# Three tiny tiles padded so that every large on-chip tile starts at a multiple of 64 bytes

## The chip, the cores and the metric

The kernel runs on one core of a Trainium2 chip. The metric is the device time of one execution in microseconds, a median over runs. One further execution was taken with the hardware profiler; all rows below are from it. The engines are PE (TensorE: matrix products), DVE (VectorE), ACT (ScalarE), POOL (GpSimd) and SP (SyncE, which here only issues transfers).

## The reference

A trunk of two decoder layers on a sequence of 512 tokens with model width 1024, all in float32. Layer 0 mixes tokens by stick-breaking attention (16 heads of width 64), layer 1 by retention (4 heads); each is followed by a squared-ReLU MLP with hidden width 4096, and there is an RMS norm before every sub-layer and at the end.

```python
def stick_breaking_attention(h, w_in, w_out):
    q, k, v = jnp.split(h @ w_in, 3, axis=-1)
    ...
    z = jnp.einsum('bhqd,bhkd->bhqk', qb, kp) * scale
    log_keep = jnp.where(mask, jax.nn.log_sigmoid(-z), 0.0)
    later = lax.cumsum(log_keep, axis=3, reverse=True) - log_keep
    a = jnp.where(mask, jnp.exp(jax.nn.log_sigmoid(z) + later), 0.0)
    outs.append(jnp.einsum('bhqk,bhkd->bhqd', a, vp))
    ...
    return o @ w_out

def reference(x, ...):
    h = x
    for layer in range(DEPTH):
        hn = rms_norm(h, g_mix[layer])
        h = h + (stick_breaking_attention if layer % 2 == 0 else retention)(hn, ...)
        h = h + squared_relu_mlp(rms_norm(h, g_mlp[layer]), ...)
    return rms_norm(h, g_final)
```

## The kernel before

Every float32 operand of a product is split into a rounded part (`hi`) and the rest (`lo`), and each product is made of three: hi by hi, hi by lo, lo by hi (`mm3_steps`, issued at line 79). The activations lie transposed (features on the 128 partitions, 512 tokens along the row), so nearly all products move 512 columns past a stationary block of 128 by 128. In the rows a product is written `out<-moving,stationary`: `so<-o,whi_so` moves the attention's output `o` past the output projection's weights, `up<-xhi,whi_up` moves the normed activations `x` past the MLP's first weights.

All products are tied into one hand-written order on PE. Layer 0 runs so: `v` (values for all heads), then `q` and `k` chains of 24 products, with the heads' work laid between pieces of them. Each head has its scores `z` (11 products: three add a mask, four move `k`, four move the split key tile `khi`, in widths 128 to 512; `weights_of`), two sigmoids on ACT, a running product and a multiplication on DVE, ten transposes `t` (line 82; the stationary operand is the weights tile `sg`) and eight products `av` that move the transposed weights `ahi` and `alo` (`turned`, `mixed`). From the 14th head on, the output projection `so` takes the place of the chains: a group of 96 products over four PSUM banks and four chains of 24, 192 in all, which move nothing but `o`. Then follow the MLP, retention (scores `rs`, its products `ro`, its output projection `rout`) and the second MLP.

On-chip memory is handed out by pools that are opened and closed like a stack. The pools `const`, `hp` (`h` and `x`), `wp` (weights: `raw`, `whi`, `wlo`) and `small` stay open to the end. On top of them lies in turn the attention's pool `sb`, the MLP's `mlp0`, retention's `ret` and `mlp1`. A tile takes its size rounded up to 32 bytes per partition, and the next one starts right behind it. In `small` lies `ssq`, of 32 bytes, and what comes behind it starts 32 bytes past a multiple of 64: the small scalars, and then every tile of the attention's pool (`q`, `k`, `hi`, `lo`, `keep`, `sg`, `ahi`, `alo`, the `vo` ring with `v` and `o`). In the MLP's pool this holds for `hT` alone, as `r2`, again 32 bytes, stands right behind it; in retention's for `cs` alone, as `minus` stands right behind it. The tiles of `const`, `hp` and `wp`, and all other large tiles, start at multiples of 64.

Of the kernel before, what the change touches and what calls it, by code (L numbers as in the profile page):

```python
# [7 lines left out]
F32 = mybir.dt.float32  # L8
# [4 lines left out]
P = 128  # L13
D = 1024
S = 512
KT = D // P
NB = S // P
# [7 lines left out]
def trunk_kernel(  # L25
# [28 lines left out]
    small = ctx.enter_context(tc.tile_pool(name="small", bufs=2))  # L54
# [484 lines left out]
    def mlp_s(layer, norm, early=None, first_up=None):  # L539
# [15 lines left out]
        with ExitStack() as st:  # L555
            mp = st.enter_context(tc.tile_pool(name=f"mlp{layer}", bufs=2, reuse_waits="tile"))
            hT = mp.tile([P, NB, D], F32, name="hT", bufs=1)
            finish = early is not None
            r2 = mp.tile([P, 2, NB], F32, name="r2", bufs=1)
            us = {}  # L560
            left, right = slice(0, 512), slice(512, D)
            low, high = slice(0, S // 2), slice(S // 2, S)
# [241 lines left out]
                    nxt.add(d)  # L804


            ssq = small.tile([P, NB, 2], F32, tag="ssq", name=f"ssq{layer}", bufs=1)
            scales = {}

            def squares(b, j):  # L810
# [71 lines left out]
    def ret_layer(norm0, norm1, early):  # L882
        w = w_ret_in
        with ExitStack() as st:
            rp = st.enter_context(tc.tile_pool(name="ret", bufs=2, reuse_waits="tile"))
            cs = rp.tile([P, 2, S], F32, name="cs", bufs=1)
            nc.scalar.dma_start(cs, rot)
            minus = rp.tile([P, KT], F32, name="minus", bufs=1)
            nc.vector.tensor_scalar(minus, gain[:, 2, :], -1.0, None, op0=ALU.mult)

            def ring(name, dtype=F32):
# [341 lines left out]
    norm, nxt = nxt, Norm("n2")  # L1233
    early = Steps(side_by_side())
    mlp_s(0, norm, early, first_up)
    norm, nxt = nxt, Norm("n3")
    ret_layer(norm, nxt, early)
    norm = nxt
    mlp_s(1, norm)


# [52 lines left out]
```

## Time and profile before

| | |
|---|---|
| median of 3 runs | 1334.22 us (1331.64 to 1334.32) |
| the profiled execution's own time | 1334.43 us |
| its span, first to last instruction | 1332.6 us |
| PE busy | 1301.3 us, 98% of the span |
| DVE, ACT, POOL busy | 71%, 49%, 11% |
| granted PE clock, mean over the span | 0.992 |

The span is what the trace shows; the 1.8 us between it and the execution's time lie before the first and after the last instruction. PE's products overlap each other by some 160 ns (a product's record lasts 389 ns, and the next one starts 227 ns after it), so the pace of PE is read from starts, not from durations.

### The profile page before, as it was taken

Reading aid. Unit: us, or ns where it says so; the run is one execution under the profiler, and the core shown is the slowest. Engines: PE = TensorE matmul, PEld = TensorE weight load, DVE = VectorE, ACT = ScalarE, POOL = GpSimd, SP = SyncE. Lnnn points to the kernel's source line nnn. Section 1 sums busy time; section 2 is a strip of 40 time slices with the busy share of each in tenths; the row PEclk is TensorE's granted clock in tenths of the full one; section 3 lists DMA queues with packets and bytes.
Section 4 is the critical chain, followed back from the end, with each engine's and each line's share of the span. In section 5 each row is a group of like instructions: output and inputs, shape, how many; then the busy total and the mean of one; then the engine's idle time right before and its main releaser. Section 6 shows DMA issues by size and latency. Waiting matters only on the chain.

```text
span 1332.6 us, 15884 instructions
## 1 busy us (share of the span) xinstructions
PE 1301.3 (98%) x5982; PEld 1076.4 (81%) x5982; DVE 939.7 (71%) x1206; ACT 652.1 (49%) x958; POOL 142.4 (11%) x162
## 2 busy tenths in 40 slices
PE   9999999999999999997999999999999999999996
PEld 7888878788888888776878788788788888888884
DVE  5778886735576575899787767677773657657588
ACT  6466664535555534554635235235254444553355
POOL 1000000110111111101011000000100011111113
PEclk9999999999999999998999999999999999999998
DMA  6455451554445354433536335334434344435324
GB/s 208 120 142 137 108 137 55 168 132 104 148 111 140 114 126 143 111 77 89 149 88 144 123 78 138 115 75 124 172 100 112 94 158 111 130 123 127 111 64 111
DMA packets 103437, 160.51 MB, mean 120 GB/s; under 512 B 6208, under 2 KB 43200, under 8 KB 103360
## 3 DMA queue, kind: packets, MB, share of 16 engines
q1 hardware_dynamic: 79648, 98.12, 23.8%
q0 software_dynamic: 22272, 58.73, 19.6%
q10 hardware_dynamic: 1440, 2.64, 0.5%
q8 instruction: 47, 0.77, 0.2%
q14 instruction: 30, 0.25, 0.1%
HBM read 146.88 MB, written 2.10 MB: 112 GB/s over the span
## 4 chain that ended last, share of the span: by engine, by line
PE 90%; DVE 7%; issue 1%; ACT 1%; DMA 1%; POOL 0%; POOLq 0%; DVEq 0%; ACTq 0%
PE up L79 26%; PE X L79 17%; PE Z L79 9%; PE k L79 7%; PE rout L79 6%; PE q L79 6%; PE Y L79 4%; PE so L79 3%; PE v L79 3%; PE z L79 2%; PE av L79 2%; PE ro L79 2%; PE t L82 1%; DVE hT L734 1%; PE rs L79 1%
## 5 line engine op out<-in xcount | busy, mean ns | idle before, releaser
L79 PE MATMUL up<-xhi,whi_up 128*128 128x512 f32 x512 | 200.1, 391 | 0.0
L79 PE MATMUL up<-xhi,wlo_up 128*128 128x512 f32 x512 | 199.4, 389 | 0.0
L79 PE MATMUL up<-xlo,whi_up 128*128 128x512 f32 x512 | 199.3, 389 | 0.0
L606 POOL DMA_DIRECT2D B<-in_w_mlp_down x92 | 82.7, 901 | 608.4 <-DVE b_1lo L110 274.1
L120 DVE TENSOR_TENSOR wlo_up<-raw_up,whi_up 128x1024 fp32r<-128x1024 f32 x64 | 78.1, 1220 | 78.1 <-ACT whi_up L119 78.0
L119 ACT CAST whi_up<-raw_up 128x1024 fp32r<-128x1024 f32 x64 | 67.4, 1052 | 95.5 <-PE up L79 82.0
L79 PEld LDWEIGHTS up<-xhi,wlo_up 128*128 128x128 f32 x512 | 96.1, 188 | 20.2
L79 PEld LDWEIGHTS up<-xhi,whi_up 128*128 128x128 f32 x512 | 96.1, 188 | 19.7
L79 PEld LDWEIGHTS up<-xlo,whi_up 128*128 128x128 f32 x512 | 96.1, 188 | 19.5
L110 DVE TENSOR_TENSOR b_1lo<-B,b_1hi 128x1024 fp32r<-128x1024 f32 x56 | 68.3, 1220 | 3.6 <-ACT b_1hi L109 3.3
L110 DVE TENSOR_TENSOR b_0lo<-B,b_0hi 128x1024 fp32r<-128x1024 f32 x56 | 68.4, 1221 | 2.3 <-ACT b_0hi L109 1.1
L109 ACT CAST b_0hi<-B 128x1024 fp32r<-128x1024 f32 x56 | 58.7, 1048 | 6.8 <-DVE B L646 2.6
L109 ACT CAST b_1hi<-B 128x1024 fp32r<-128x1024 f32 x56 | 58.8, 1050 | 6.6 <-DVE B L650 3.5
L591 ACT ACTIVATE U<-up 128x512 f32<-128x512 f32 x64 | 36.5, 592 | 37.6 <-PE up L79 37.6
L79 PE MATMUL q<-xlo,whi_q 128*128 128x512 f32 x128 | 51.5, 403 | 1.5 <-DVE xlo L264 1.5
L79 PE MATMUL k<-xhi,wlo_k 128*128 128x512 f32 x128 | 51.2, 400 | 0.0
L79 PE MATMUL q<-xhi,whi_q 128*128 128x512 f32 x128 | 50.8, 397 | 0.2 <-ACT xhi L263 0.2
L79 PE MATMUL k<-xlo,whi_k 128*128 128x512 f32 x128 | 50.8, 397 | 0.0
L79 PE MATMUL k<-xhi,whi_k 128*128 128x512 f32 x128 | 50.5, 395 | 0.0
L110 DVE TENSOR_TENSOR a_1lo<-S,a_1hi 128x512 fp32r<-128x512 f32 x24 | 16.5, 688 | 48.1 <-ACT a_1hi L109 48.1
L79 PE MATMUL q<-xhi,wlo_q 128*128 128x512 f32 x128 | 50.3, 393 | 0.0
L79 PE MATMUL rout<-yhi,whi_rout 128*128 128x512 f32 x128 | 50.1, 392 | 0.0
(389 smaller groups left out, 3349.3 us busy)
## 6 DMA issues: line engine op xcount, KB each, us to landing
B<-in_w_mlp_down POOLq DMA_DIRECT2D x96, 512.0 KB, 5.1
raw_up<-in_w_mlp_up SPq DMA_DIRECT2D x64, 512.0 KB, 3.9
B<-in_w_ret_in SPq DMA_DIRECT2D x24, 512.0 KB, 3.9
raw_rout<-in_w_ret_out SPq DMA_DIRECT2D x16, 512.0 KB, 3.6
raw_q<-in_w_sb_in SPq DMA_DIRECT2D x8, 512.0 KB, 4.4
raw_k<-in_w_sb_in SPq DMA_DIRECT2D x8, 512.0 KB, 4.3
q<-hi SPq DMA_DIRECT2D x32, 128.0 KB, 3.4
raw_so<-in_w_sb_out SPq DMA_DIRECT2D x8, 512.0 KB, 3.9
```

Source lines behind the costliest of these rows:

```text
L79: pe(nc.tensor.matmul(o, a, b, start=start, stop=stop, **kw))
L82: pe(nc.tensor.transpose(o, a, ident))
L109: nc.scalar.copy(hi, src_ap)
L110: (eng or nc.vector).tensor_tensor(lo, src_ap, hi.bitcast(F32), op=ALU.subtract)
L119: nc.scalar.copy(hi, raw)
L120: (sub or nc.vector).tensor_tensor(lo, raw, hi.bitcast(F32), op=ALU.subtract)
L591: nc.scalar.activation(U[:, m, :], banks[m], AF.Relu)
L606: nc.gpsimd.dma_start(t[:, ks, :], src[:, ks, :], **kw)
L734: nc.vector.scalar_tensor_tensor(at, acc[b], by, at, op0=ALU.mult, op1=ALU.add)
```

## The change

Three tiles get twice the bytes that they use, and their first half is used as before: `ssq` and `minus` take 64 bytes in place of 32, and `r2` takes 64 in place of 32.

```diff
@@ -556,7 +556,7 @@
             hT = mp.tile([P, NB, D], F32, name="hT", bufs=1)
             finish = early is not None
-            r2 = mp.tile([P, 2, NB], F32, name="r2", bufs=1)
+            r2 = mp.tile([P, 2, 2 * NB], F32, name="r2", bufs=1)[:, :, 0:NB]
@@ -804,7 +804,8 @@
-            ssq = small.tile([P, NB, 2], F32, tag="ssq", name=f"ssq{layer}", bufs=1)
+
+            ssq = small.tile([P, NB, 4], F32, tag="ssq", name=f"ssq{layer}", bufs=1)[:, :, 0:2]
@@ -885,7 +886,7 @@
-            minus = rp.tile([P, KT], F32, name="minus", bufs=1)
+            minus = rp.tile([P, 2 * KT], F32, name="minus", bufs=1)[:, 0:KT]
```

No instruction is added, removed or moved on any engine, and no shape changes. What changes is where tiles lie. Start bytes in the built programs, and what is left of them after division by 64:

| tile | before | after |
|---|---|---|
| `xhi0` (pool `hp`) | 34112, 0 | 34112, 0 |
| `whi` (pool `wp`), first buffer | 79168, 0 | 79168, 0 |
| `o0` (attention) | 147744, 32 | 147776, 0 |
| `q0_0` (attention) | 188704, 32 | 188736, 0 |
| `ahi_0_0` (attention) | 211232, 32 | 211264, 0 |
| `hT` (MLP) | 114464, 32 | 114496, 0 |
| `U0_0` (MLP) | 130880, 0 | 130944, 0 |
| `cs` (retention) | 114464, 32 | 114496, 0 |
| `dec0` (retention) | 118592, 0 | 118656, 0 |

## Rows read from the trace of the kernel before

**Rows 1.** The page: the span, the busy time of three engines with their share and number of instructions, and the shares of the chain of work that ended last, by engine.

```profile
span 1332.6 us, 15884 instructions
PE 1301.3 (98%) x5982; PEld 1076.4 (81%) x5982; DVE 939.7 (71%) x1206; ACT 652.1 (49%) x958; POOL 142.4 (11%) x162
...
PE 90%; DVE 7%; issue 1%; ACT 1%; DMA 1%; POOL 0%; POOLq 0%; DVEq 0%; ACTq 0%
```

**Rows 2.** PE's waits over the whole span: the waiting product, what released it, then us in total, times, longest.

```profile
PE rbps_n L79 <- DVE diag_n L252: 6.6, 1, 6.6
...
PE t L82 <- ACT sg L415: 2.1, 1, 2.1
...
PE z L79 <- DMA k<-lo: 1.2, 1, 1.2
```

**Rows 3.** PE's timeline inside the output projection: start in us, length in us, the products merged where neighbours are alike. In this stretch rows come in turn with one and with two products, so a row with two comes every three products.

```profile
231.97 0.63 PE L79 MATMUL so<-o,whi_so 128*128 128x512 f32 x2
...
234.77 0.63 PE L79 MATMUL so<-o,whi_so 128*128 128x512 f32 x2
```

**Rows 4.** The same timeline in the first MLP, one product in each row; between the two rows lie 25 more.

```profile
257.79 0.39 PE L79 MATMUL up<-xhi,whi_up 128*128 128x512 f32 x1
...
263.68 0.39 PE L79 MATMUL up<-xhi,wlo_up 128*128 128x512 f32 x1
```

**Rows 5.** Pieces of the chain that ended last, in order of time: start in us, us, what, number of products.

```profile
231.20 10.05 PE so L79 x43
...
627.16 5.44 PE X L79 x24
```

**Rows 6.** Groups of products that move 512 columns, over the whole span: number, busy us, mean ns of one, idle time before.

```profile
L79 PE MATMUL up<-xlo,whi_up 128*128 128x512 f32 x512 | 199.3, 389 | 0.0
...
L79 PE MATMUL so<-o,whi_so 128*128 128x512 f32 x128 | 42.2, 409 | 0.2 <-ACT whi_so L119 0.2
```

**Rows 7.** The output projection's tile `so`: shortest, median and longest duration in ns.

```profile
L79 PE MATMUL so<-o,whi_so x128: 388/396/632, 197.8 to 255.9; 128*128 128x512 f32 x128
...
L79 PE MATMUL so<-o,wlo_so x64: 392/395/632, 198.4 to 256.2; 128*128 128x512 f32 x64
```

**Rows 8.** The heads' products from 66 to 242 us, shapes kept apart: number, busy us, mean ns of one.

```profile
L79 PE MATMUL z<-hi,qlo 128*128 128x512 f32 x16 | 6.3, 395 | 0.0
L79 PE MATMUL av<-ahi,v 128*128 128x512 f32 x16 | 6.3, 395 | 0.0
L79 PE MATMUL av<-alo,v 128*128 128x512 f32 x16 | 6.3, 395 | 0.0
L79 PE MATMUL av<-alo,v 128*128 128x384 f32 x16 | 5.4, 340 | 0.0
L79 PE MATMUL z<-k,q 128*128 128x384 f32 x16 | 5.4, 337 | 0.0
...
L79 PE MATMUL av<-alo,v 128*128 128x256 f32 x16 | 4.5, 279 | 0.0
L79 PE MATMUL av<-alo,v 128*128 128x128 f32 x16 | 4.4, 274 | 0.0
```

**Rows 9.** Retention's scores from 640 to 650 us, whose tiles start at multiples of 64, in the same columns.

```profile
L79 PE MATMUL rs<-q0lo,k0hi 128*128 128x384 f32 x2 | 0.7, 338 | 0.0
...
L79 PE MATMUL rs<-q0lo,k0hi 128*128 128x256 f32 x2 | 0.6, 280 | 0.0
...
L79 PE MATMUL rs<-q0hi,k0lo 128*128 128x128 f32 x2 | 0.5, 274 | 0.0
```

**Rows 10.** PE's timeline behind transposes, in the second MLP (all tiles at multiples of 64); between the two rows lie four products.

```profile
1015.17 0.39 PE L79 MATMUL up<-xlo,whi_up 128*128 128x512 f32 x1
...
1016.33 0.39 PE L79 MATMUL up<-xhi,whi_up 128*128 128x512 f32 x1
```

**Rows 11.** The same behind a head's transposes in the attention, where the chain's own operands start at multiples of 64; between the two rows lie nine products.

```profile
101.94 0.40 PE L79 MATMUL q<-xhi,wlo_q 128*128 128x512 f32 x1
...
104.25 0.39 PE L79 MATMUL q<-xhi,whi_q 128*128 128x512 f32 x1
```

**Rows 12.** Stretches around the two places at which the granted clock is low: from and to in us, length, then busy us and instructions of PE, weight loads, DVE, ACT and POOL, granted clock (1.00 is 2.4 GHz), DMA share, GB/s.

```profile
195.20:197.10 1.90, 0.00 (x0) 0.00 (x0) 1.80 (x2) 1.90 (x6) 1.53 (x1) 1.00 0.97 280
...
198.50:202.00 3.50, 3.50 (x10) 2.72 (x9) 3.41 (x5) 0.29 (x2) 0.00 (x0) 0.51 0.49 112
...
611.10:617.70 6.60, 0.04 (x1) 0.03 (x1) 6.53 (x16) 1.55 (x2) 1.19 (x1) 0.53 0.00 0
617.70:621.80 4.10, 4.10 (x8) 2.60 (x9) 4.10 (x5) 1.86 (x3) 0.22 (x1) 0.50 0.00 0
```

**Rows 13.** PE's timeline in the first of these places; from the first row's start to the last row's lie six products.

```profile
198.61 1.06 PE L79 MATMUL so<-o,whi_so 128*128 128x512 f32 x2
...
201.17 0.99 PE L79 MATMUL so<-o,whi_so 128*128 128x512 f32 x2
```

**Rows 14.** Other engines, over the whole span: DVE's subtraction into a tile of the attention (`alo`) and into one of retention (`ylo`), and weight loads of transposes whose stationary tile is the attention's `sg` or retention's `y`.

```profile
L110 DVE TENSOR_TENSOR alo<-t,ahi 128x512 fp32r<-128x512 f32 x32 | 21.0, 681 | 3.4 <-ACT ahi L109 3.3
...
L82 PEld LDWEIGHTS t<-ident,sg 128*128 128x128 f32 x160 | 18.3, 140 | 4.5 <-ACT sg L415 2.3 <-DVE oF L465 0.2
...
L110 DVE TENSOR_TENSOR ylo<-yt,yhi 128x512 fp32r<-128x512 f32 x16 | 11.0, 688 | 10.6 <-ACT yhi L109 10.6
...
L82 PEld LDWEIGHTS yt<-ident,y 128*128 128x128 f32 x64 | 8.0, 140 | 2.1
```

## The prediction, made before the changed kernel ran

> **What bounds the kernel.** I read the page first: PE is busy for 98% of the span and holds 90% of the chain that ended last; no other engine is above 71% [rows 1]. PE's waits over the whole span are few: 6.6 us at one norm, 2.1 us for one head's transposes, 1.2 us for one transfer [rows 2]. So time that a product gives up on PE before one of these waits is time that the kernel gives up, as long as what ends the wait moves with PE. It does: the longest ones in the attention end with ACT work on PSUM banks that PE has just filled, and the norm's wait starts from PE's own last sums. A busy PE can still be a slow PE, so I next read its pace from starts in the timeline, in the stretches where like products follow each other.
>
> There the two kinds of tiles part. In the output projection, 12 products lie between the starts 231.97 and 234.77 [rows 3]: 2.80 us / 12 = 233.3 ns each. In the first MLP, 26 steps lie between 257.79 and 263.68 [rows 4]: 5.89 / 26 = 226.5 ns. The chain's pieces say the same over longer stretches: 43 products of `so` in 10.05 us are 233.7 ns, 24 of retention's `X` in 5.44 us are 226.7 ns [rows 5]. All move 512 columns past 128 by 128, all take weights from the same `whi` and `wlo` buffers or like ones, and PE waits for nothing in these stretches. The durations agree: medians of 396 and 395 ns in `so` [rows 7], against a mean of 389 in `up`. (The mean of 409 in `so` holds the products at the low clock [rows 6].) What `so` has apart from the others is that its moving tile `o` starts 32 bytes past a multiple of 64. The step is 233.3 - 226.7 = 6.7 ns, and at 2.4 GHz that is 16 cycles, the time of 16 columns, which are 64 bytes. I read this as one more piece of 64 bytes that a moving row touches when it starts in the middle of one: 33 pieces in place of 32.
>
> [...]
>
> **The change part by part.** No instruction comes or goes, so the sum is over products whose moving tile moves to a multiple of 64.
>
> *The output projection.* 128 + 64 = 192 products [rows 7]. Eight ran at the low clock, where six take 2.56 us, 427 ns each [rows 13], which is 512 columns at 1.2 GHz and no more; these have no step to lose. 184 x 6.7 ns = 1.23 us at most. Behind transposes or short products, aligned products are slow for a while too: five steps in 1.16 us, 27 ns more than five at 226.7 [rows 10]. The projection begins anew some eight times, behind transposes, short products or a stop, so 8 x 27 ns = 0.22 us stay. That leaves 1.01, and I take 1.0 us.
>
> *The heads' products of 512 columns.* Two of `z` and two of `av` in each of 16 heads, 64 in all. Three of the four kinds average 395 ns [rows 8], 6 over 389 (the fourth stands behind the mask's product and is longer): at most 64 x 6 = 0.38 us. At least 0, since they stand behind short products, where aligned ones are slow as well. I take 0.2.
>
> *The heads' shorter products.* 15 a head, 240. At 384 columns `av` and `z` take 340 and 337 ns [rows 8], retention's aligned scores 338; at 256 columns 279 against 280; at 128 columns 274 against 274 [rows 9]. I take 0. The far bound is the full step on each, 240 x 6.7 = 1.6 us.
>
> *The chains between the heads.* Their own operands do not move, but they follow moved ones. Behind transposes ten steps of `q` take 2.31 us, 43 ns over ten at 226.7 [rows 11], where the second MLP lost 27 [rows 10]. With 25 such places, 25 x 16 ns = 0.4 us at most, and 0 at least, as the transposes themselves change nothing. I take 0.1.
>
> *Stationary tiles, DVE, ACT, transfers.* Weight loads take 140 ns from the attention's `sg` and from retention's aligned `y`; DVE's subtraction takes 681 ns into the attention's tile and 688 into the aligned one [rows 14]. So I see nothing to win there. If DVE became 7 ns slower per instruction, that would lie beside PE's products everywhere but in the last microseconds, where some ten instructions are 0.1 us. `hT` and `cs` are never moving operands, so the MLPs and retention keep their times. Transfers end a wait of PE once, 1.2 us [rows 2]; I price them at 0, since their length and number stay.
>
> Sum: 1.0 + 0.2 + 0 + 0.1 = 1.3 us, from 1.0 with the others at 0 to 1.23 + 0.38 + 1.6 + 0.4 = 3.6 us. The profiled execution took 1334.43 us, a span of 1332.6 and 1.8 around it, and lies 0.2 us above the median of the runs. 1334.4 - 1.3 = **1333.1 us**. The runs of the kernel before spread over 2.7 us, 0.2%, which is also about what a measurement can tell from no change: the gain forecast, 0.1%, lies within it.
>
> **What the clock may add.** PE's clock is granted at 1.2 GHz in two places: from 198.5 to 202 us, right after PE stood idle from 195.2 to 197.1, and around the norm's wait, where PE restarts at 617.7 and stays at half speed until 621.8 [rows 12]. The first costs half of 3.4 us, 1.7 us; the second half of 4.1 us, 2.05 us. The change moves PE's stops earlier, the first by some 0.3 us, the second by the whole 1.3.
>
> **The rivals.**
> 1. *The change does nothing*: the 6.7 ns belong to something else in `so`, for instance to a slow pace behind short products that never ends there. 1334.4 us. For it: chains of aligned tiles also run slow behind short products [rows 11], so a slow pace alone does not prove a start address. Against it: those recover within ten products or so, and `so` does not in 43 [rows 5]. Chance 0.10. [...]
> 2. *Every moving product gains*, the short ones and all: 192 + 304 = 496 x 6.7 = 3.3 us, 1331.1 us. Against it stands that [rows 8, 9] agree at equal widths. Chance 0.08.
> 3. *The clock comes back sooner.* If the first low stretch goes, another 1.7 us; if the second ends sooner by two microseconds of its four, another 1.0: 1333.1 less that is 1331.4 to 1332.1. For it: the first low stretch follows a stop of only 2.1 us, so it may hang on little. Chance 0.17.
> 4. *The clock stays low for longer* (the other side). PE restarts from the norm 1.3 us sooner; if the clock comes back at the same moment as before, these 1.3 us run at half speed and 0.65 of the gain is lost: 1333.8. If one more stretch of 3.4 us is granted at 1.2 GHz, it costs 1.7, more than the whole gain: 1334.8, slower than before. It decides from an added 2.6 us at half speed on; to be slower by over 0.2% it takes 2.7 + 1.3 = 4.0 us of loss, 8 us more at 1.2 GHz. Chance 0.07 for a result above 1334, and 0.03 of it over 0.2%.
>
> **How the numbers follow.** The forecast itself has 0.58; its own range, from 0.9 to 2.0 us of gain (`so` alone, or with the wide products and the chains in full), is 1332.4 to 1333.5. The range that holds 8 in 10 takes in the third rival, the nothing case and the second one's edge: 1330.9 to 1334.7. Faster by over 0.2%, below 1331.8 by the profiled execution: the second rival, half of the third and a little of the first case's edge, 0.08 + 0.08 + 0.02 = 0.18. Slower by over 0.2%: 0.03. The rest, 0.79, is within.
>
> **What would show it.** Right: in the changed trace `so` steps by 226.7 ns with a median of 389, the piece of 43 products takes 9.75 us in place of 10.05, and the heads' 512-column products fall to near 389 while the narrower ones, DVE's and ACT's instructions stay. Wrong in the first step: `so` still at 233. Wrong in the zero for the narrow products: 384-column `av` under 334 ns. If the step goes and the time does not, I would look at the granted clock behind 195 and 611 us first, then for a new wait of PE for DVE between 246 and 257 us, where the projection ends.

## The result: slower by 0.5%, and the profile after

The changed kernel takes 1341.57 us (median of six runs, 1340.46 to 1343.78), the kernel before 1335.45 (six runs, 1331.64 to 1336.69): a ratio of 1.0050, 95% interval 1.0034 to 1.0067. Here and below a ratio compares all the runs, so it can differ a little from the quotient of the two medians that stand beside it. The forecast was 1333.1 with a range up to 1334.7. The profiled execution took 1340.46 us, 6.0 more than that of before.

The page of the changed kernel, first the lines that answer to [rows 1], then groups of products (number, busy us, mean ns of one, idle time before):

```profile
span 1338.7 us, 15884 instructions
...
PE 1309.4 (98%) x5982; PEld 1076.1 (80%) x5982; DVE 940.5 (70%) x1206; ACT 651.6 (49%) x958; POOL 142.7 (11%) x162
...
PE 89%; DVE 7%; ACT 1%; issue 1%; DMA 0%; POOL 0%; POOLq 0%; ACTq 0%; DVEq 0%
...
L79 PE MATMUL up<-xhi,whi_up 128*128 128x512 f32 x512 | 201.4, 393 | 0.0
L79 PE MATMUL up<-xlo,whi_up 128*128 128x512 f32 x512 | 200.7, 392 | 0.0
```

The span grew by 6.1 us and PE's busy time by 8.1, with the same 5982 instructions. DVE, ACT and POOL are within 1 us. PE's waits did not grow, as its waits over the whole span show beside [rows 2]:

```profile
PE rbps_n L79 <- DVE diag_n L252: 6.6, 1, 6.6
...
PE t L82 <- ACT sg L415: 2.0, 1, 2.0
...
PE z L79 <- DMA k<-lo: 0.3, 1, 0.3
```

So PE does the same work at a slower pace, and one place is already in sight: `xlo` past `whi_up` took 389 ns in [rows 6] and takes 392, and neither of its two tiles was moved. Pieces of the chain that ended last (start, us, what, number of products) give the pace over longer stretches:

```profile
228.49 9.79 PE so L79 x43
...
626.62 5.44 PE X L79 x24
632.06 5.60 PE Z L79 x24
637.66 5.60 PE X L79 x24
```

The output projection did what was forecast: 9.79 us / 43 = 227.7 ns in place of 233.7 [rows 5]. But retention now has pieces of 24 products at 5.60 us, 233.3 ns, which is the slow step that `so` had before. These are the products whose stationary operand is `form`, a tile of retention's pool.

Where the 6.1 us arose is read from the first and the last start of one kind of product in each stage. For the changed kernel, by tile (number, shortest, median and longest ns, first and last start), first MLP, second MLP, retention's first `form` products, retention's output:

```profile
L79 PE MATMUL up<-xhi,wlo_up x256: 388/389/397, 253.6 to 540.6; 128*128 128x512 f32 x128
L79 PE MATMUL up<-xhi,wlo_up x256: 388/389/398, 989.8 to 1280.7; 128*128 128x512 f32 x128
L79 PE MATMUL Z<-b50hi,form x32: 393/396/398, 631.9 to 901.1; 128*128 128x512 f32 x32
L79 PE MATMUL rout<-yhi,wlo_rout x128: 388/389/397, 745.8 to 989.1; 128*128 128x512 f32 x128
```

The same rows of the kernel before:

```profile
L79 PE MATMUL up<-xhi,wlo_up x256: 389/389/397, 256.9 to 540.9; 128*128 128x512 f32 x128
L79 PE MATMUL up<-xhi,wlo_up x256: 389/389/398, 986.8 to 1274.6; 128*128 128x512 f32 x128
L79 PE MATMUL Z<-b50hi,form x32: 389/389/389, 632.4 to 899.0; 128*128 128x512 f32 x32
L79 PE MATMUL rout<-yhi,wlo_rout x128: 388/389/398, 744.8 to 986.1; 128*128 128x512 f32 x128
```

The attention's side gives 3.3 us (`up` starts at 253.6 in place of 256.9). The first MLP takes 287.0 in place of 284.0 (+3.0). Retention, from the first `Z` to the last `rout`, takes 357.2 in place of 353.7 (+3.5). The second MLP takes 290.9 in place of 287.8 (+3.1). Together, -3.3 + 3.0 + 3.5 + 3.1 = +6.3, and the last `up` starts 6.1 us later.

In the first MLP the loss sits where two groups of products alternate. PE's timeline of the changed kernel (start, length), first product of a group of nine `up`, first of the six `X` behind it, and first of the next nine:

```profile
350.08 0.39 PE L79 MATMUL up<-xhi,whi_up 128*128 128x512 f32 x1
...
352.15 0.39 PE L79 MATMUL X<-b_0hi,a_0hi 128*128 128x512 f32 x1
...
353.53 0.39 PE L79 MATMUL up<-xhi,whi_up 128*128 128x512 f32 x1
```

The same block in the kernel before:

```profile
352.80 0.39 PE L79 MATMUL up<-xhi,whi_up 128*128 128x512 f32 x1
...
354.84 0.39 PE L79 MATMUL X<-b_0hi,a_0hi 128*128 128x512 f32 x1
...
356.20 0.39 PE L79 MATMUL up<-xhi,whi_up 128*128 128x512 f32 x1
```

15 products take 3.45 us, 230.0 ns each, where they took 3.40, 226.7 each. The longest stretch of the stage in which `up` stands alone keeps its pace: 159 products from 269.0 us on before, from 265.7 us on after, 227.6 ns each in both. So here neither kind of product is slow by itself.

### The profile page after: what moved, and what is told of

Same layout as the page of the kernel before. It is cut to its first block, busy times and chain, and to the rows that moved or that the text cites. A ratio compares the mean times of both kernels' runs of the same rounds, so it can differ in the third digit from the quotient of the medians.

```text
span 1338.7 us, 15884 instructions
## 1 busy us (share of the span) xinstructions
PE 1309.4 (98%) x5982; PEld 1076.1 (80%) x5982; DVE 940.5 (70%) x1206; ACT 651.6 (49%) x958; POOL 142.7 (11%) x162
## 4 chain that ended last, share of the span: by engine, by line
PE 89%; DVE 7%; ACT 1%; issue 1%; DMA 0%; POOL 0%; POOLq 0%; ACTq 0%; DVEq 0%
PE up L79 26%; PE X L79 17%; PE Z L79 9%; PE k L79 7%; PE rout L79 6%; PE q L79 5%; PE Y L79 4%; PE v L79 3%; PE so L79 3%; PE z L79 2%; PE ro L79 2%; PE av L79 1%; PE t L82 1%; DVE hT L734 1%; PE rs L79 1%
```

## What the runs tell apart

Start bytes explain both losses, but not by the rule of the prediction. In the kernel before, the tiles that the long chains read outside the attention start 64 bytes past a multiple of 256 (`xhi0` 34112, `whi` 79168, `U0_0` 130880, `dec0` 118592), so the starts of a moving and of a stationary operand differ by a multiple of 256. (`hT` and `cs`, at 32 past, are not read by these chains.) The attention's tiles start 32 past one, so for `so` the difference, moving minus stationary, is 224 modulo 256. The change moves the attention to 64, beside the rest; but it also moves the MLP's and retention's tiles from 64 to 128, away from `x` and the weights, which stay. I call "distance" this difference modulo 256. The theory is then: at distance 0 a 512-column product steps by 226.7 ns, at most others by more, and a change between groups that lie at different places costs something too, even where each group has distance 0.

The expectations below name the theories by letters. A is that the distance decides, with a period of 128 or more that was still open; A2 is A with the period 256. B is that each tile's own place decides, 64 past a multiple of 128. C is that the loss comes from something else in the changed kernel. The prediction's own rule (a moving row that starts off a multiple of 64 is slow) is tested at the end.

**Larger pads in the MLP and in retention.** `r2` and `minus` take 128 bytes, which puts the tiles behind them at 192 modulo 256, 128 from `x`. Against the changed kernel:

```diff
-            r2 = mp.tile([P, 2, 2 * NB], F32, name="r2", bufs=1)[:, :, 0:NB]
+            r2 = mp.tile([P, 2, 4 * NB], F32, name="r2", bufs=1)[:, :, 0:NB]
-            minus = rp.tile([P, 2 * KT], F32, name="minus", bufs=1)[:, 0:KT]
+            minus = rp.tile([P, 4 * KT], F32, name="minus", bufs=1)[:, 0:KT]
```

> The changed kernel with r2 and minus at 128 bytes in place of 64, so that the attention's, the MLPs' and retention's large tiles all start 64 bytes past a multiple of 128, as h, x and the weight tiles do. Theory A (what counts is the distance between the start of the moving tile and that of the stationary tile, modulo 128 or more; equal is fast): so steps by 226.7 ns, the MLPs and retention step by 226.7 again as before the change; 1.3 to 3.3 us faster than the kernel before, 7 to 9 us faster than the changed kernel. Theory B (each tile by itself must lie 64 bytes past a multiple of 128): the same numbers. Theory C (the step by multiples of 64 was right and the loss comes from something else in the changed kernel, such as moved transfers or DVE): the loss of some 9 us in the MLPs and retention stays.

Measured 1339.44 us against 1333.64, ratio 1.0043 (1.0031 to 1.0056). It is still slower, so equality modulo 128 is not enough, and A with the period 128 falls. The `form` products, now at distance 128, step by 232.2 ns.

**Everything moved by 64 bytes.** A tile in the first pool moves all that lies behind it. Against the kernel before:

```diff
     gain = const.tile([P, 4, KT], F32, name="gain")
+    front = const.tile([P, 16], F32, name="front")
+    nc.vector.memset(front, 0.0)
```

> The kernel before with one more tile of 64 bytes in the constants' pool, ahead of all large tiles. Every large tile moves by 64 bytes and no distance between two of them changes. Theory A: same time as before within 0.1%, so still at 233.3 ns, up at 226.7. Theory B: tiles that lay at 64 modulo 128 now lie at 0, and nearly all products slow down to 229 ns or more: 1% slower, some 13 us. Theory C: same time.

Measured 1333.76 against 1333.64, ratio 1.0001 (0.9992 to 1.0010). The MLPs lie in this kernel where they lie in the changed one, to the byte modulo 256, and lose nothing: the first takes 284.1 us, and `so` keeps its 10.05.

```profile
228.87 10.05 PE so L79 x43
...
L79 PE MATMUL up<-xhi,wlo_up x256: 389/389/397, 254.5 to 538.6; 128*128 128x512 f32 x128
```

So their absolute place does not count, and B, which expected some 13 us, falls.

**`r2` alone at 128 bytes,** the other pads as in the changed kernel:

```diff
-            r2 = mp.tile([P, 2, 2 * NB], F32, name="r2", bufs=1)[:, :, 0:NB]
+            r2 = mp.tile([P, 2, 4 * NB], F32, name="r2", bufs=1)[:, :, 0:NB]
```

> The changed kernel with r2 alone at 128 bytes: the MLPs' tiles lie at 64 modulo 128 again, retention's stay at 0. Theories A and B: the MLPs step by 226.7 ns and give back some 3.0 us each, retention keeps its loss of some 3.3 us: 1335.6 us where the changed kernel has 1341.6, about the time of the kernel before. Theory C: as the changed kernel.

Measured 1339.25, ratio 1.0041 (1.0026 to 1.0055). The MLPs come back only in part at 128 from `x`, to 285.3 and 289.1 us, where the changed kernel has 287.0 and 290.9 and the kernel before 284.0 and 287.8. The number expected, 1335.6, was missed; with the products of zeros below, this made 256 the next size to try.

```profile
L79 PE MATMUL up<-xhi,wlo_up x256: 389/389/397, 255.5 to 540.8; 128*128 128x512 f32 x128
```

**The pace by itself.** Behind the end of the last layer (with the 128-byte pads) stand products of zeros, whose results are not used, with no other engine at work: 24 of 512 columns at each of 16 distances, then alternating places, then groups of nine and six.

```diff
+            def run(name, n, at):
+                o = bank(f"pr_{name}", "a")
+                for i in range(n):
+                    m, s = at(i)
+                    s += 512 * (i % 2)
+                    mm(o, big[:, s // 4 : s // 4 + P], big[:, m // 4 : m // 4 + S], True, True, ...)
...
+            for d in DISTANCES:
+                run(f"d{d}", 24, lambda i: (far + d, 0))
...
+            for r in range(4):
+                run(f"long{r}", 9, lambda i: (far, 0))
+                run(f"short{r}", 6, lambda i: (far + 64, 64))
```

> The kernel of e_all128 with some 900 products of a tile of zeros behind its end (their results are not used; the total time means nothing). Each run of 24 products moves 512 columns past 128 by 128 with a set distance in bytes between the moving and the stationary start. Theory A: 226.7 ns at distance 0, 233.3 at -32 or +224, 233.4 at +192 (-64), 229.0 at +64, and back to 226.7 at some period of 128, 256 or 512; the runs with both starts moved by 64 step like those without. In runs that alternate, one of the two orders (own pair equal, or moving equal to the next product's stationary) is slow: if the load of the next stationary tile is what collides, the order with equal own pairs is slow and the other at 226.7. Theory B: the runs with both starts moved by 64 step otherwise than those without, and distance alone decides nothing. Runs of 9 and 6 products at two places, as in the MLP, lose some 3 ns per product over 226.7 by A.

Groups of these products in five windows, in the order of the distances 0, 32, 64, 192 and 256 (number, busy us, mean ns):

```profile
L80 PE MATMUL pr_d<-big 128*128 128x512 f32 x23 | 5.4, 389 | 0.0
L80 PE MATMUL pr_d<-big 128*128 128x512 f32 x23 | 5.5, 395 | 0.0
L80 PE MATMUL pr_d<-big 128*128 128x512 f32 x23 | 5.4, 392 | 0.0
L80 PE MATMUL pr_d<-big 128*128 128x512 f32 x23 | 5.5, 394 | 0.0
L80 PE MATMUL pr_d<-big 128*128 128x512 f32 x18 | 4.2, 389 | 0.0
```

Distances 0 and 256 give 389 ns, the others more, and the starts say the same: 226.7 ns at 0, 256, 512 and 1024; 228.9 at 64 and 320; 233.2 at 32; 233.3 at 192 and 448. With both starts moved by 64 each distance keeps its pace (226.7 at 0, 233.3 at 32, 228.9 at 64, 233.5 at 192). So it is the difference that counts, and 256 is its period. The groups of nine and six, whose places lie 64 apart while each group has distance 0, in the timeline:

```profile
1516.44 2.23 PE L80 MATMUL pr_long<-big 128*128 128x512 f32 x9
1518.50 1.54 PE L80 MATMUL pr_short<-big 128*128 128x512 f32 x6
1519.89 0.39 PE L80 MATMUL pr_long<-big 128*128 128x512 f32 x1
```

15 products in 3.45 us, 230.0 ns: the MLP's loss, made with zeros and without DVE, ACT or transfers beside it. One expectation failed: of the two orders of alternating places one was to step by 226.7 ns, and both are slow (last section).

**All at one place.** If distance is the cause, the attention can be brought to 64 modulo 256 without moving any other tile that the long chains read: `r2` and `minus` leave the MLP's and retention's pools and share one buffer of 32 bytes in `small`. It moves everything behind `small` by 32, and in the MLP and retention only `hT` and `cs` feel it, as the 32 bytes of `r2` and `minus` behind them are gone. Against the kernel before:

```diff
-            r2 = mp.tile([P, 2, NB], F32, name="r2", bufs=1)
+            r2 = small.tile([P, 2, NB], F32, tag="aux", name=f"r2{layer}", bufs=1)
-            minus = rp.tile([P, KT], F32, name="minus", bufs=1)
+            minus = small.tile([P, KT], F32, tag="aux", name="minus", bufs=1)
```

> The kernel before with r2 and minus taken out of the MLP's and retention's pools and put into small, in one buffer of 32 bytes behind ssq. So the attention's tiles, hT and cs move by 32 bytes, and every other large tile stays where it was before the change: all tiles that PE reads in wide products start 64 bytes past a multiple of 256. Theory A2 (what counts is that the moving and the stationary start are equal modulo 256): so steps by 226.7 ns, the MLPs and retention step by 226.7 as before; 1.0 to 1.3 us faster than before (0.1%, hardly to be told from no change), 6 to 8 us faster than the changed kernel. Theory C (the loss of the changed kernel comes from something else than the pairs): some loss against the kernel before stays.

Measured 1331.84 against 1333.84, ratio 0.9990 (0.9981 to 0.9998). This is the fastest of the kernels here, by little. Its chain and its stages:

```profile
230.14 9.79 PE so L79 x43
```

```profile
L79 PE MATMUL up<-xhi,wlo_up x256: 389/389/397, 255.2 to 539.3; 128*128 128x512 f32 x128
L79 PE MATMUL up<-xhi,wlo_up x256: 389/389/398, 984.9 to 1272.7; 128*128 128x512 f32 x128
L79 PE MATMUL Z<-b50hi,form x32: 389/389/389, 630.5 to 897.1; 128*128 128x512 f32 x32
L79 PE MATMUL rout<-yhi,wlo_rout x128: 388/389/398, 742.9 to 984.2; 128*128 128x512 f32 x128
```

`so` is as fast as in the changed kernel, and the stages last 284.1, 353.7 and 287.8 us, as before. The gain of the change is there without its loss. The interval only just leaves out no change; that the gain is there apart from the clock is read product by product in the section on the prediction.

**`ssq` alone padded,** which moves the MLP's and retention's tiles to 96 modulo 256, 32 from `x` and the weights:

```diff
-            ssq = small.tile([P, NB, 2], F32, tag="ssq", name=f"ssq{layer}", bufs=1)
+            ssq = small.tile([P, NB, 4], F32, tag="ssq", name=f"ssq{layer}", bufs=1)[:, :, 0:2]
```

> The first of the three paddings alone (ssq at 64 bytes, r2 and minus at 32): the attention's tiles at 64 past a multiple of 256, the MLPs' and retention's at 96, x and the weights at 64. Theory A2: the attention is as fast as in the changed kernel; the MLPs lose some 3 us each at the changes between the two kinds of products, as in the changed kernel; retention's products of forms (stationary 32 past) and its output projection (moving 32 past) step by 233 ns, 384 products each, 2.6 + 2.5 us: 8 to 10 us slower than before. A theory by which only a distance of 64 hurts has the MLPs and retention at 226.7 and the kernel 1 us faster than before.

Measured 1342.12, ratio 1.0071 (1.0057 to 1.0085), 8.3 us slower by the medians. The two MLPs lose what they lose in the changed kernel (286.7 and 290.5). Retention takes 358.7 us, 5.0 more than before: `form` at distance 224 steps by 233.3 ns and `rout` at 32 by 233.3, where the changed kernel's `rout` at distance 64 steps by 229.0.

**`r2` at 256 bytes** (`8 * NB`), so that the MLP's tiles come to 64 modulo 256 again; retention as in the changed kernel.

> The changed kernel with r2 at 256 bytes: the MLPs' tiles lie at 64 modulo 256 again, as x and the weights do; retention's lie at 128 as in the changed kernel. Theory A2: both MLPs step by 226.7 ns without a break, 6 us come back; retention's loss of some 3.3 us stays: 1 to 3 us slower than before. Theory C: as the changed kernel, 6 us slower than before.

Measured 1335.31, ratio 1.0018 (1.0009 to 1.0027). By tile:

```profile
L79 PE MATMUL up<-xhi,wlo_up x256: 389/389/397, 255.7 to 539.7; 128*128 128x512 f32 x128
L79 PE MATMUL up<-xhi,wlo_up x256: 389/389/397, 989.1 to 1277.0; 128*128 128x512 f32 x128
L79 PE MATMUL Z<-b50hi,form x32: 393/396/398, 631.0 to 900.3; 128*128 128x512 f32 x32
```

The MLPs are back at 284.0 and 287.9 us, and retention keeps its loss (357.4, with the last `rout` at 988.4).

**The counterpart: retention put right, the MLPs not.** Against the changed kernel `ssq` gets its 32 bytes back and `minus` goes into `small`:

```diff
-            ssq = small.tile([P, NB, 4], F32, tag="ssq", name=f"ssq{layer}", bufs=1)[:, :, 0:2]
+            ssq = small.tile([P, NB, 2], F32, tag="ssq", name=f"ssq{layer}", bufs=1)
-            minus = rp.tile([P, 2 * KT], F32, name="minus", bufs=1)[:, 0:KT]
+            minus = small.tile([P, KT], F32, tag="aux", name="minus", bufs=1)
```

> The changed kernel with minus moved into small (ssq back at 32 bytes, so that nothing else moves): retention's tiles lie 64 past a multiple of 256 again, as x and the weights do; the MLPs' lie at 128 as in the changed kernel. Theory A2: the counterpart of the run with r2 at 256 bytes: retention steps by 226.7 ns, the MLPs keep their loss of some 6 us: 1339 us, 4 to 6 us slower than before. Together with that run the two losses should add up to that of the changed kernel plus the attention's gain of 1 us, some 9 us.

Measured 1338.48, ratio 1.0042 (1.0028 to 1.0055). By tile:

```profile
L79 PE MATMUL up<-xhi,wlo_up x256: 388/389/397, 254.6 to 541.5; 128*128 128x512 f32 x128
L79 PE MATMUL Z<-b50hi,form x32: 389/389/389, 632.9 to 899.4; 128*128 128x512 f32 x32
```

`form` is back at 389 ns and retention at 353.7 us; the MLPs keep 286.9 and 290.7. The two losses are separate, each with its tiles: 2.9 + 2.9 us in the MLPs here and 3.7 in retention in the run before this one are 9.5, where the changed kernel loses 3.0 + 3.5 + 3.1 = 9.6.

**Everything moved by 32 bytes,** for the prediction's own rule: the `front` tile of above with 8 columns in place of 16, so that outside the attention only `hT` and `cs`, of the large tiles, start at a multiple of 64.

> The kernel before with one more tile of 32 bytes in the constants' pool, ahead of all large tiles: the attention's tiles now start at multiples of 64, and x, the weights and nearly all tiles of the MLPs and of retention start 32 bytes past one. No distance between two large tiles changes. Theory of the prediction (a moving row that starts 32 bytes past a multiple of 64 costs 6.7 ns more): so falls to 226.7 ns, and some 5000 other products of 512 columns rise to 233.3, 33 us or 2.5% slower. Theory A2 (the distance modulo 256 between the moving and the stationary start decides, not where either lies): same time as before within 0.1%, so at 233.3 and the others at 226.7.

Measured 1333.52 against 1333.40, ratio 1.0002 (0.9993 to 1.0010). Some 5000 wide products now have a moving row that starts in the middle of 64 bytes, and their chains keep their pace: the first MLP takes 284.0 us. `so`, whose `o` now starts at a multiple of 64, keeps its 10.05 us:

```profile
230.80 10.05 PE so L79 x43
...
L79 PE MATMUL up<-xhi,wlo_up x256: 389/389/397, 256.5 to 540.5; 128*128 128x512 f32 x128
```

The prediction's rule falls.

**More distances, widths and bf16,** products of zeros behind the end as above, on the fastest kernel:

```diff
+            for cols in (384, 256, 128):
+                for d in (0, 32, 64, 128, 192):
+                    run(f"w{cols}d{d}", 32, lambda i: (far + d, 0), cols)
...
+            for d in (0, 16, 32, 64, 128, 192, 256):
+                run(f"b{d}", 32, lambda i: (far // 2 + d, 0), S, half)
```

> The kernel of e_same256 with some 1100 products of zeros behind its end (results not used; the total time means nothing). Distances of 4, 8, 80, 112, 240 and 252 bytes between the moving and the stationary start: A2 expects all over 226.7 ns, near 233 from 32 on, less at 4 and 8 if the slow step grows with the distance as it did from 16 to 32. Runs in which only the moving or only the stationary start alternates between two places: at 256 apart 226.7, at 32, 64 and 128 apart over 228 in both, if equality of a pair is what counts; if one of the two kinds is at 226.7, that side is free. Narrower products (384, 256, 128 columns): a loss of 0 to 6.7 ns at unequal starts; in the kernel before none was seen at 32. bf16: not known; 0 if the effect belongs to rows of 4-byte elements.

Its numbers stand in the last section.

## Why the prediction was wrong, point by point

**The step of `so` was real, its cause was not.** The working went from a true reading, 233.3 against 226.7 ns with `o` 32 bytes off, to "one more piece of 64 bytes that a moving row touches". The match of 6.7 ns with 16 columns carried it (427 ns for 512 columns at half the granted clock [rows 12, 13] make 6.7 ns for 16 at the full one). That a row is read in pieces of 64 bytes was the author's estimate, which no run shows; nothing in the trace of before showed a long chain with another start or another distance to try it on. Moving everything by 32 bytes shows no cost of a start by itself (ratio 1.0002, `so` still at 10.05 us); the distance to the stationary operand, 224 in `so`, makes the step.

**From it came the step that failed:** "`hT` and `cs` are never moving operands, so the MLPs and retention keep their times". It looked only at the tiles that were off a multiple of 64, and only at moving operands. But the MLP's and retention's other tiles moved too, from 64 to 128 modulo 256, as the start bytes of `U0_0` and `dec0` say, and `x` and the weights did not. In retention that pulls the two operands of `form`'s and `rout`'s products apart. In the MLPs each product keeps distance 0, but the MLP's own products (`X`, `Z`) now alternate with `up` between two places. That costs +3.0 us in the first MLP, +3.5 in retention and +3.1 in the second MLP. Retention's part is accounted for by its products: 384 with `form` at 233.3 in place of 226.7 ns are 2.6 us, 384 of `rout` at 229.0 are 0.9. In the first MLP 873 products stand in alternating groups of six or nine, at 229.8 in place of 226.7 ns: 2.7 of the 3.0 us, and the longer groups between them lose another 0.2.

**The gain came, at some two thirds of its size, and by luck.** `so` steps by 226.7 ns: from the first row to the last of this timeline of the changed kernel lie 12 products, 2.72 us, where [rows 3] had 2.80.

```profile
232.66 0.62 PE L79 MATMUL so<-o,whi_so 128*128 128x512 f32 x2
...
235.38 0.39 PE L79 MATMUL so<-o,whi_so 128*128 128x512 f32 x1
```

Its median is 389, as forecast, and the 43 products took 9.79 us where 9.75 was said. That is luck as far as the reason goes: the pad brought `o` to 64 modulo 256, where the weights lie, and a multiple of 64 alone would not have done it, as `rout` at distance 64 shows with 229.0 ns. Of the 3.3 us by which the MLP starts sooner, 0.9 is a transfer that ended its wait earlier and 1.6 the first stretch at the low clock (0.51 from 198.5 to 202 us [rows 12]), and neither belongs to the change: in the kernel with everything moved by 64 bytes, where `so` keeps its 233.3 ns, the transfer's wait ends earlier too (by 0.7), the granted clock is full from 195 to 210 us as well, and the MLP starts 2.4 us sooner than before. The row of the changed kernel, then that of the moved one (granted clock third from the end):

```profile
195.00:210.00 15.00, 13.70 (x75) 11.89 (x76) 12.33 (x14) 8.20 (x18) 0.88 (x1) 1.00 0.32 84
```

```profile
195.00:210.00 15.00, 13.63 (x74) 11.70 (x75) 12.17 (x13) 8.27 (x18) 0.92 (x1) 1.00 0.33 88
```

What is left, 3.3 - 0.9 - 1.6 = 0.8 us, is the change's, against 1.3 forecast. It stands apart from the clock: the products that run from 204 to 257.5 us in the kernel before take 0.7 to 0.8 us less in each of the kernels in which `o` lies beside the weights, and the same to within 0.01 us in the two in which everything moved together. The second stretch at the low clock (granted 0.50 from 617.7 to 621.8 us before [rows 12], 0.57 in the same window after) changed little in time: from the last `up` of the first MLP to retention's first `Z` it is 91.5 us before and 91.3 after.

**The heads gave less than said.** The 0.3 us for their 512-column products and the chains between them is not there: from 82 to 182 us the changed kernel gains 0.06 us. The products' own rows stay close to [rows 8]:

```profile
L79 PE MATMUL z<-hi,qlo 128*128 128x512 f32 x16 | 6.3, 395 | 0.0
L79 PE MATMUL av<-ahi,v 128*128 128x512 f32 x16 | 6.3, 394 | 0.0
L79 PE MATMUL av<-alo,v 128*128 128x512 f32 x16 | 6.3, 393 | 0.0
```

Among themselves the heads' operands always lay at distance 0: both are tiles of the attention. So there was nothing to win by the distance. That they take 395 ns all the same may come from the short products before them, as products at distance 0 lose time behind transposes too (27 ns in five steps [rows 10]); no run here varies that. The zeros for narrow products, DVE and ACT held: `av<-alo` takes 338, 281 and 273 ns at 384, 256 and 128 columns, where it took 340, 279 and 274 [rows 8], DVE's subtraction into `alo` 682 ns in place of 681, a weight load from `sg` 140 as before [rows 14], and ACT's busy time went from 652.1 to 651.6 us. So did the zero for transfers, as the earlier end of the wait came without the change too.

**The rivals.** All four went by the start bytes of moving tiles or by the clock. None was a loss in tiles that the change moves and the forecast left out. The chance of 0.03 for slower by over 0.2% hung on the clock alone, and the loss came with a granted clock that was no lower than before (0.995 against 0.992, mean over the span).

## What to carry to other kernels

When a change moves tiles, list for every long kind of product where both operands start, before and after, and ask which pairs move against each other; a tile that "becomes aligned" may do so by leaving its partners. A step that shows for one pair of tiles alone has at least two readings, the start of one and the distance of both, and a shift of everything by the same amount tells them apart in one run. Small tiles that share a buffer in a pool of their own leave the large ones behind them where they are.

## What the runs showed of the hardware

The pace of a float32 product of 512 columns in this kernel's rounded form (`F32R`, from start to start, settled; mean granted clock of the two runs with products of zeros 0.993 and 0.992) depends on the distance in bytes between the starts of its moving and stationary operand, in the distances taken with period 256. In the products of zeros, the mean over the last 15 steps of each run of 24, each distance taken once:

| distance | ns | distance | ns |
|---|---|---|---|
| 0, 256, 512, 1024 | 226.7 | 112, 252 | 226.7 |
| 64, 320 | 228.9 | 80 | 231.1 |
| 16 | 231.5 | 384 | 232.9 |
| 8, 32, 48, 96, 192, 224, 448 | 233.2 to 233.5 | 128, 160 | 233.6, 234.3 |
| 4, 240 | 236.6, 236.5 | | |

Alternating the moving start alone between two places costs too (231.7 ns at 32 apart, 231.0 at 64, 229.8 at 128, 226.7 at 256), and so does alternating the stationary one (235.0, 230.2, 232.3, 226.7). At 384 columns the steps are 173.3 ns at distances 0, 32 and 64 and 176 to 177 at 128 and 192; at 256 columns distance 0 is the slowest, 120.0 against 113.4 at 192; at 128 columns all are 111.5 to 111.7. In the kernels' own chains the same distances give 233.3 ns (192, 224 and 32) and 229.0 (64), as with zeros, but 232.2 to 232.3 at 128. In bf16 at 512 columns none of the distances taken shows: seven of them, from 0 to 256, lie in one row of the timeline, 224 products in 48.2 us, and behind the first product each step is 215 or 216 ns.

```profile
1520.61 48.52 PE L80 MATMUL pr_b<-half 128*128 128x512 bf16 x219
1568.78 5.82 PE L80 MATMUL pr_again<-big 128*128 128x512 f32 x24
```

(Five of their records are missing, and the step across such a gap is twice as long.) That the distance counts, and a common shift of 32 or 64 bytes does not (ratios 1.0002 and 1.0001), says that the pace hangs on both starts together. By what mechanism, and between which operands, no run here shows: alternating both starts in the same or in opposite order is slow either way (231.7 and 230.0 ns at 32 apart, 231.7 and 231.6 at 64). Why 112 and 252 step by 226.7, against what was expected, stays open too.
